# An encoder block on one core: x loaded over two queues, transposed blocks paired differently in PSUM, four gate sigmoids and one weight cut moved

## The chip, the cores and the metric

The kernel runs on one core of a Trainium2 chip. The metric is device microseconds of one execution, taken as the median of several runs. A separate profiled execution gives the trace from which all durations below come. Engine names: PE is TensorE's matmul side and PEld its weight load, DVE is VectorE, ACT is ScalarE, POOL is GpSimd and SP is SyncE, which only issues transfers here.

## The reference

One layer with sequence length 256 and model width 1024, all in float32:

```python
h = rmsnorm(x, norm_gain)
a_in, a_gate, q, k, v, b_gp, g_logits = split(h @ w_in)          # 1024 -> 8192 columns
y_a = (multiscale_pool(a_in, w_pool, pool_scale) * silu(a_gate)) @ w_proj_a
y_b = (dilated_attention(q, k, v, rel_bias) * silu(b_gp)) @ w_proj_b
gates = sigmoid(g_logits + b_gate)                               # two gates of 1024 columns
merged = gates[0] * y_a + gates[1] * y_b
y = rmsnorm(x + merged @ w_out, final_gain)
```

`multiscale_pool` takes centred means over windows of 2, 4, 8 and 16 positions in four groups of 128 channels, subtracts the token and multiplies each group by its own 128 x 128 matrix. The attention has 24 heads of 64 in three groups with different dilation; the eight heads of a group are merged over the groups by their softmax denominators.

## The kernel before, in words

**Exact products from rounded halves.** PE multiplies in a rounded 32-bit type (fp32r). To keep float32 accuracy every operand is cut into a high part (a rounding copy, `whi` for weights, `hh` for activations) and a low part (the rest, `wlo`, `hl`), and every product is three matmuls: high by high, low by high and high by low (`mm3`, lines 246 to 249). The high part of a weight tile is written by ACT (line 128), its low part by DVE (line 133); both are done in `cut_half`, half a tile at a time, two tiles ahead of the matmuls that use it. Weights come from DRAM in 41 tiles of `order` (lines 82 to 90), mostly 1 MB, through four raw buffers (`wraw`) on SP's queue; there are three buffers of `whi` and `wlo`, so the ACT copy of tile n waits until PE has finished tile n-3. The tile of kind `pool` holds the four 128 x 128 matrices; its halves have 2 x 128 columns each, and line 130 cuts its low part into four pieces of 128 x 128.

**The head (lines 68 to 243).** Its instructions on ACT, DVE, PE and POOL run in the order in which they are written. X, 256 rows by 1024, is loaded as two row blocks of 128 rows (512 KB each), both from SP's queue and ahead of the weights; the parameters `prm` come on ACT's queue. For each row block b, ACT and DVE each sum the squares of one half (lines 185, 187), DVE adds the sums (line 190), POOL takes the power -1/2 (line 191), and DVE and ACT scale one half of the row block each into `XN` (lines 194, 195). DVE then makes the high part of weight tile 0 in two halves (line 197), and POOL its low part in two pieces (lines 199, 200). `turn(kc, b)` transposes channel block kc (128 of the 1024 channels) of row block b on PE. The results go to four PSUM tiles `tps[0]` to `tps[3]`, one bank each, and every bank holds two channel blocks: kc and kc + 4 (line 204). For each kc, ACT reads the block from PSUM and writes its high part `hh` (line 223), and DVE reads the same block and `hh` and writes the low part `hl` (line 224). Between these, PE runs the first projection (`part0`, 16 matmuls for each of the three products): the product with `hl[kc]` two steps behind that with `hh[kc]`; then, when all of `hl` is used, the product with `wlo` with three small bias matmuls in between (line 237). PE's first matmul after the head is that of line 247.

**The long middle.** `heads` projects k, q and v, `project_t` gives one accumulator per 128 output channels from three PSUM banks (`mmb`, tag "mm"), and `step` (line 353) advances the attention: a scores stage `stage_s` (ends with an Exp on ACT, line 304), a transposing stage `stage_t` and an output stage `stage_o`. The latter ends with an ACT copy (line 344) and two DVE additions (lines 345, 346) that empty a single PSUM bank `op`. Outside the head the order on each engine is laid down when the program is built: an instruction that comes earlier in the text goes first if the builder's own model takes it to be ready; dependencies can be added by hand. `behind` adds such a dependency: a Sigmoid never goes ahead of the latest `stage_o` copy traced before it, because Exp and Sigmoid lie in different tables of ACT.

**The end of the middle.** Eight gate tiles (`gate_tile`, line 565) give the gate logits: tiles 0 to 3 fill `GA`, branch A's gate, tiles 4 to 7 branch B's. Each tile has two accumulators, each copied out by ACT (line 572), a `cut_half` and a `step`. After gate tile 6 come four pooling products (`mx`, line 595) and their scaling on DVE (line 597), the split of their result (lines 600, 601), a cut of the next weight tile and gate tile 7. Then the remaining attention steps run, and `squash` (line 604) applies Sigmoid in place to the two halves of `GA`, line 606. Branch A (`branch`, line 613) forms eight accumulators `y`; DVE multiplies each by its block of `GA` (`done_a`, line 629), which frees the PSUM bank that the third next accumulator needs. Branch B, the output product, the residual and the final norm follow.

Of the kernel before, what the change touches and what calls it, by code (L numbers as in the profile page):

```python
# [11 lines left out]
F32 = mybir.dt.float32  # L12
F32R = mybir.dt.float32r
AF = mybir.ActivationFunctionType
ALU = mybir.AluOpType
PSUM = bass.MemoryType.PSUM

P = 128
# [24 lines left out]
def encoder_block(ctx: ExitStack, tc: tile.TileContext, x, w_in, lines, w_pool, w_proj_a, w_proj_b,  # L43
                  w_out, final_gain, params, out):
    nc = tc.nc
    x2 = x[0]
# [6 lines left out]
    def slot(shape, dt, tag, name, bufs=1):  # L53
        return sb.tile(shape, dt, tag=tag, name=name, bufs=bufs)
# [6 lines left out]
    def bank(shape, tag, name, bufs):  # L61
        return ps.tile(shape, F32, tag=tag, name=name, bufs=bufs)
# [4 lines left out]

    X = slot([P, 2, D], F32, "v", "X", 2)
    for b in range(2):
        nc.sync.dma_start(X[:, b, :], x2[b * P:(b + 1) * P, :])  # L70
    ident = sb.tile([P, P], F32, name="ident")
    make_identity(nc, ident)
    mhalf = sb.tile([P, 1], F32, name="mhalf")
# [8 lines left out]
    order = []  # L82
# [12 lines left out]
    def load_next():  # L95
        n = state["load"]
        if n >= len(order):
            return
        kind, c = order[n]
        if kind == "in":  # L100
            src, shp = w_in[c // 256], [8, 256]
        elif kind == "pool":
            src, shp = w_pool, [4, 128]
        else:
            src, shp = {"pa": w_proj_a, "pb": w_proj_b, "out": w_out}[kind][c], [4, 512]
        t = slot([P] + shp, F32, "wraw", f"wraw{n}", NRAW)
        if n == 0:
            for h in range(2):
                k = shp[0] // 2
                nc.sync.dma_start(t[:, h * k:(h + 1) * k, :], src[:, h * k:(h + 1) * k, :])  # L110
        else:
            nc.sync.dma_start(t, src)
        raws[n] = (t, shp)
        state["load"] = n + 1

    def cut_half():
        n, h = divmod(state["cut"], 2)
        if n >= len(order):
            return
        t, shp = raws[n]  # L120
        if h == 0:
            parts[n] = (slot([P] + shp, F32R, "whi", f"whi{n}", 3), slot([P] + shp, F32R, "wlo", f"wlo{n}", 3))
            if n:
                load_next()
        hi, lo = parts[n]
        k = shp[0] // 2
        s = slice(h * k, (h + 1) * k)
        nc.scalar.activation(hi[:, s, :], t[:, s, :], AF.Copy)  # L128

        m = (k + 1) // 2 if 9 <= n <= 18 or n >= 24 else k  # L130
        for q in range(h * k, (h + 1) * k, m):
            s = slice(q, q + m)
            nc.vector.tensor_tensor(lo[:, s, :], t[:, s, :], hi[:, s, :].bitcast(F32), op=ALU.subtract)  # L133
        state["cut"] += 1

    def cut_next():
        cut_half()
        cut_half()

    def weights(n):  # L140
        return parts.pop(n)
# [13 lines left out]
    XN = slot([P, 2, D], F32, "v", "XN", 2)  # L155
# [5 lines left out]
    def cut_lo(n, k0, k1, eng):  # L161
        t, (hi, lo) = raws[n][0], parts[n]
        return eng.tensor_tensor(lo[:, k0:k1, :], t[:, k0:k1, :], hi[:, k0:k1, :].bitcast(F32), op=ALU.subtract)

    def open_parts(n):
        shp = raws[n][1]
        parts[n] = (slot([P] + shp, F32R, "whi", f"whi{n}", 3), slot([P] + shp, F32R, "wlo", f"wlo{n}", 3))
        state["cut"] = 2 * n + 2

    with tc.manual_schedule(engines={mybir.EngineType.Activation, mybir.EngineType.DVE, mybir.EngineType.PE,  # L170
                                    mybir.EngineType.Pool}):
        tiny = sb.tile([P, 1], F32, name="tiny")
        warm = sb.tile([P, P], F32, name="warm")
        nc.vector.memset(warm, 0.0)
        nc.scalar.activation(tiny, warm[:, 0:1], AF.Square)

        def keep_warm(times):
            for _ in range(times):
                nc.tensor.matmul(misc[:, P:2 * P], warm, warm, start=True, stop=True)

        keep_warm(WARM)
        halves = [slice(h * 512, (h + 1) * 512) for h in range(2)]
        for b in range(2):
            sq = [slot([P, 512], F32, "st", f"sq{b}{h}", 3) for h in range(2)]
            nc.scalar.activation(sq[0], X[:, b, halves[0]], AF.Square, scale=1.0 / 32.0, accum_out=ss[:, b, 0:1])
            xb = X[:, b, halves[1]]
            nc.vector.tensor_tensor_reduce(sq[1], xb, xb, scale=1.0 / D, scalar=EPS, op0=ALU.mult, op1=ALU.add,
                                           accum_out=ss[:, b, 1:2])
            t = slot([P, 1], F32, "rt", f"rt{b}", 2)
            nc.vector.tensor_tensor(t, ss[:, b, 0:1], ss[:, b, 1:2], op=ALU.add)  # L190
            nc.gpsimd.tensor_tensor(rs[:, b:b + 1], t, mhalf, op=ALU.pow)
        open_parts(0)
        for b in range(2):
            nc.vector.tensor_scalar(XN[:, b, halves[0]], X[:, b, halves[0]], rs[:, b:b + 1], None, op0=ALU.mult)
            nc.scalar.activation(XN[:, b, halves[1]], X[:, b, halves[1]], AF.Copy, scale=rs[:, b:b + 1])
        for k in (0, 4):
            nc.vector.tensor_copy(parts[0][0][:, k:k + 4, :], raws[0][0][:, k:k + 4, :])

        cut_lo(0, 0, 5, nc.gpsimd)
        first_lo = cut_lo(0, 5, 8, nc.gpsimd)  # L200
        tps = [bank([P, 2, S], "mm" if i < 3 else "T", f"tp{i}", 3 if i < 3 else 2) for i in range(4)]

        def turn(kc, b):
            nc.tensor.transpose(tps[kc % 4][:, kc // 4, b * P:(b + 1) * P], XN[:, b, kc * P:(kc + 1) * P], ident)

        acc = bank([P, 2, 512], "S", "k00", 1)
        acc0 = [acc[:, u, 0:S] for u in range(2)]

        def part0(kc, x):
            hi_, lo_ = parts[0]  # L210
            for u in range(2):
                c = slice(u * P, (u + 1) * P)
                nc.tensor.matmul(acc0[u], (lo_ if x == 2 else hi_)[:, kc, c], (hl if x == 1 else hh)[:, kc, :],
                                 start=x == 0 and kc == 0, stop=x == 2 and kc == KC - 1)

        for kc in range(KC):
            turn(kc, 0)
        for kc in range(KC):
            turn(kc // 2 + kc % 2 * 4, 1)
        for kc in range(KC):  # L220
            v = tps[kc % 4][:, kc // 4]
            gcol = prm[:, kc:kc + 1]
            nc.scalar.activation(hh[:, kc, :], v, AF.Copy, scale=gcol)
            nc.vector.scalar_tensor_tensor(hl[:, kc, :], v, gcol, hh[:, kc, :].bitcast(F32), op0=ALU.mult,
                                           op1=ALU.subtract)
            part0(kc, 0)
            if kc >= 2:
                part0(kc - 2, 1)
        for kc in (6, 7):
            part0(kc, 1)  # L230
        for kc in range(KC):
            if kc == 5:

                for t in range(3):
                    w = 3 * NH
                    o = 3 * P + t // 2 * w
                    nc.tensor.matmul(misc[:, t * w:(t + 1) * w], oh[:, t * P:(t + 1) * P], oh[:, o:o + w],
                                     start=True, stop=True)
            part0(kc, 2)
        cut_next()  # L240
        nc.vector.tensor_copy(line.rearrange("p i r h -> p r i h"),
                              misc[:, 0:LROW * NH].rearrange("p (r i h) -> p r i h", i=2, h=4))
        cut_next()
# [14 lines left out]
    def project_t(hi, lo, cb, name):  # L258
        acc = mmb(name)
        c = slice(cb * P, (cb + 1) * P)  # L260
        for kc in range(KC):
            mm3(acc, hi[:, kc, c], lo[:, kc, c], hh[:, kc, :], hl[:, kc, :], kc == 0, kc == KC - 1)
        return acc
# [111 lines left out]
    n = 0  # L375

    def heads(I, parts_):
        nonlocal n
        for part in parts_:
            for g in range(NG):  # L380
                hi, lo = weights(n) if n else (None, None)
                for u in range(2):
# [46 lines left out]
                    if n:  # L429
                        cut_half()  # L430
# [67 lines left out]
    for dst in ("u", "a", "b"):  # L498
        for t in range(2):
            hi, lo = weights(n)  # L500
# [61 lines left out]
    GA = GG[:, 0:8]  # L562
    GB = [GG[:, 8 + i] for i in range(4)]

    def gate_tile(t):
        nonlocal n
        hi, lo = weights(n)
        for u in range(2):
            cb = (2 * t + u) % 8
            acc = project_t(hi, lo, u, f"g{t}{u}")  # L570
            i = 8 + 2 * t + u
            nc.scalar.activation(GA[:, cb] if t < 4 else GB[cb], acc, AF.Identity, bias=prm[:, i:i + 1])
            cut_half()
            step()
        n += 1
# [28 lines left out]
    def squash(G):  # L604
        for g in G:
            behind(nc.scalar.activation(g, g, AF.Sigmoid), last_exp[0])

    gate_tile(7)
    while live:
        step()  # L610
    squash((GA[:, 0:4], GA[:, 4:8]))

    def branch(src_h, src_l, done):
        nonlocal n
# [208 lines left out]
```

## Time and profile before

| | |
|---|---|
| median of 3 runs | 260.43 us (260.27 to 260.70) |
| the profiled execution's own time | 260.82 us |
| its span | 259.0 us |
| PE busy | 250.4 us in 2160 matmuls |
| DVE busy | 210.2 us |
| ACT busy | 164.4 us |
| POOL busy | 74.5 us |
| memory read and written | 47.42 MB and 1.09 MB |
| granted PE clock | 0.995 of full speed over the span |

How to read it: the span goes from the first to the last instruction of the profiled execution, and 1.82 us of its own time lie outside. A row of the timeline gives the start in us, the duration in us, engine, line, operation, output<-inputs, shape and the count of merged instructions; in square brackets stands how long the engine had been idle before it and what ended that. Durations of neighbours on one engine overlap: the copy of line 223 lasts 0.47 us, but the next one begins 0.36 to 0.39 us after it. A row of the waits names who waited for whom, then the total, the times and the longest in us.

### The profile page before, as it was taken

How to read it: one execution, taken by the hardware profiler on the slowest of the kernel's cores; microseconds unless marked ns; L12 is line 12 of the kernel's file. 1: busy time of each engine (PE TensorE's matmuls, PEld its weight loads, DVE VectorE, ACT ScalarE, POOL GpSimd, SP SyncE). 2: the span in 40 equal slices, each digit the busy share in tenths (PEclk: the TensorE clock that was granted, in tenths of full speed). 3: DMA queues.
4: the chain of work that ended last, by engine and by line, in shares of the span. 5: the costliest groups of instructions: out<-in, count | busy, mean ns of one | idle time of the engine just before them, and what ended most of it. 6: DMA issues, size and time to landing. Idle time of an engine off the chain costs nothing.

```text
span 259.0 us, 5482 instructions
## 1 busy us (share of the span) xinstructions
PE 250.4 (97%) x2160; PEld 248.8 (96%) x2160; DVE 210.2 (81%) x412; ACT 164.4 (63%) x285; POOL 74.5 (29%) x101
## 2 busy tenths in 40 slices
PE   7899999999999999999999999999999999999990
PEld 7899999999999999999999999999999999999990
DVE  2899988778888787889697997967859988899383
ACT  4878577565666565658967777765457797446141
POOL 1563386002798000010763910000010020442011
PEclk9999999999999999999999999999999999999998
DMA  6999999984445553444989867144440696300022
GB/s 231 393 412 363 239 323 329 313 306 162 166 162 172 235 172 156 162 164 162 284 254 257 278 216 273 47 164 162 164 162 6 209 383 233 148 4 0 0 84 81
DMA packets 9992, 52.01 MB, mean 201 GB/s; under 512 B 1147, under 2 KB 2142, under 8 KB 4718
## 3 DMA queue, kind: packets, MB, share of 16 engines
q1 hardware_dynamic: 7022, 44.08, 48.4%
q0 software_dynamic: 2512, 7.12, 11.1%
q10 hardware_dynamic: 432, 0.46, 0.5%
q8 instruction: 17, 0.28, 0.4%
q14 instruction: 9, 0.07, 0.1%
HBM read 47.42 MB, written 1.09 MB: 187 GB/s over the span
## 4 chain that ended last, share of the span: by engine, by line
PE 84%; DVE 6%; issue 3%; ACT 2%; DMA 2%; POOLq 0%; POOL 0%; SPq 0%; DVEq 0%; ACTq 0%
PE v L249 4%; PE v L248 4%; PE q L249 4%; PE q L248 4%; PE v L247 4%; PE q L247 4%; PE g L247 4%; PE g L248 4%; PE g L249 4%; PE k L247 4%; PE k L249 4%; PE k L248 4%; PE y L247 2%; PE y L248 2%; PE y L249 2%
## 5 line engine op out<-in xcount | busy, mean ns | idle before, releaser
L133 DVE TENSOR_TENSOR wlo<-wraw,whi 128x512 fp32r<-128x512 f32 (+2 forms) x134 | 108.5, 849 | 8.3 <-ACT whi L128 7.3
L128 ACT ACTIVATE whi<-wraw 128x1024 fp32r<-128x1024 f32 (+1 forms) x80 | 81.0, 1038 | 23.2 <-PE q L248 10.1
L247 PE MATMUL g<-hh,whi 128*128 128x256 f32 x128 | 35.8, 280 | 0.0
L249 PE MATMUL g<-hh,wlo 128*128 128x256 f32 x128 | 35.4, 277 | 0.0
L248 PE MATMUL g<-hl,whi 128*128 128x256 f32 x128 | 35.4, 276 | 0.0
L304 ACT ACTIVATE st<-st,nm 128x512 f32<-128x512 f32 x16 | 11.6, 722 | 29.6 <-DVE nm L301 29.6
L247 PE MATMUL v<-whi,hh 128*128 128x256 f32 x96 | 26.6, 277 | 0.0
L249 PE MATMUL v<-whi,hl 128*128 128x256 f32 x96 | 26.5, 276 | 0.0
L248 PE MATMUL v<-wlo,hh 128*128 128x256 f32 x96 | 26.5, 276 | 0.0
L249 PE MATMUL q<-hh,wlo 128*128 128x256 f32 x96 | 26.5, 276 | 0.0
L247 PE MATMUL q<-hh,whi 128*128 128x256 f32 x96 | 26.5, 276 | 0.0
L248 PE MATMUL q<-hl,whi 128*128 128x256 f32 x96 | 26.5, 276 | 0.0
L247 PEld LDWEIGHTS g<-hh,whi 128*128 128x128 f32 x128 | 24.0, 188 | 0.1
L248 PEld LDWEIGHTS g<-hl,whi 128*128 128x128 f32 x128 | 24.1, 188 | 0.0
L249 PEld LDWEIGHTS g<-hh,wlo 128*128 128x128 f32 x128 | 24.0, 188 | 0.0
L247 PE MATMUL k<-hh,whi 128*128 128x256 f32 x80 | 22.2, 277 | 0.0
L249 PE MATMUL k<-hh,wlo 128*128 128x256 f32 x80 | 22.1, 277 | 0.0
L248 PE MATMUL k<-hl,whi 128*128 128x256 f32 x80 | 22.1, 277 | 0.0
L248 PEld LDWEIGHTS v<-wlo,hh 128*128 128x128 f32 x96 | 18.0, 188 | 0.0
L249 PEld LDWEIGHTS q<-hh,wlo 128*128 128x128 f32 x96 | 18.0, 188 | 0.0
L248 PEld LDWEIGHTS q<-hl,whi 128*128 128x128 f32 x96 | 18.0, 188 | 0.0
L247 PEld LDWEIGHTS q<-hh,whi 128*128 128x128 f32 x96 | 18.0, 188 | 0.0
(177 smaller groups left out, 760.2 us busy)
## 6 DMA issues: line engine op xcount, KB each, us to landing
wraw<-in_w_in_dram SPq DMA_DIRECT2D x31, 1024.0 KB, 6.4
wraw<-in_w_out_dram SPq DMA_DIRECT2D x4, 1024.0 KB, 4.9
T<-line_d POOLq DMA_DIRECT2D x4, 576.0 KB, 6.8
KX<-KX POOLq DMA_DIRECT2D x8, 256.0 KB, 14.5
wraw<-in_w_proj_a_dram SPq DMA_DIRECT2D x2, 1024.0 KB, 4.7
wraw<-in_w_proj_b_dram SPq DMA_DIRECT2D x2, 1024.0 KB, 4.9
X<-in_x_dram SPq DMA_DIRECT2D x2, 512.0 KB, 4.2
wraw<-in_w_in_dram SPq DMA_DIRECT2D x2, 512.0 KB, 6.6
```

Source lines behind the costliest of these rows:

```text
L128: nc.scalar.activation(hi[:, s, :], t[:, s, :], AF.Copy)
L133: nc.vector.tensor_tensor(lo[:, s, :], t[:, s, :], hi[:, s, :].bitcast(F32), op=ALU.subtract)
L247: nc.tensor.matmul(acc, ah, bh, start=first, stop=False)
L248: nc.tensor.matmul(acc, ah, bl, start=False, stop=False)
L249: nc.tensor.matmul(acc, al, bh, start=False, stop=last)
L304: e = nc.scalar.activation(st, st, AF.Exp, bias=nm, scale=-1.0, accum_out=l)
```

## The change

Five places change.

1. Row block 1 of X is issued by ACT, row block 0 by SP as before. ACT issues it ahead of `prm`.
2. The transposes of channel blocks 2j and 2j + 1 go to the same PSUM tile `tps[j]`; before, kc and kc + 4 shared one.
3. The transposes of row block 1 are issued in the order 0 to 7; before, in the order 0, 4, 1, 5, 2, 6, 3, 7, in which banks are finished one by one.
4. The low part of the tile of kind `pool` is written by POOL, all others by DVE as before.
5. `squash` of branch A's gate stands ahead of gate tile 7 and the last attention steps, not behind them.

```diff
     for b in range(2):
-        nc.sync.dma_start(X[:, b, :], x2[b * P:(b + 1) * P, :])
+        (nc.sync, nc.scalar)[b].dma_start(X[:, b, :], x2[b * P:(b + 1) * P, :])
...
         t, shp = raws[n]
+        kind = order[n][0]
...
-            nc.vector.tensor_tensor(lo[:, s, :], t[:, s, :], hi[:, s, :].bitcast(F32), op=ALU.subtract)
+            (nc.gpsimd if kind == "pool" else nc.vector).tensor_tensor(lo[:, s, :], t[:, s, :],
+                                                                       hi[:, s, :].bitcast(F32), op=ALU.subtract)
...
-            nc.tensor.transpose(tps[kc % 4][:, kc // 4, b * P:(b + 1) * P], XN[:, b, kc * P:(kc + 1) * P], ident)
+            nc.tensor.transpose(tps[kc // 2][:, kc % 2, b * P:(b + 1) * P], XN[:, b, kc * P:(kc + 1) * P], ident)
...
         for kc in range(KC):
-            turn(kc // 2 + kc % 2 * 4, 1)
+            turn(kc, 1)
         for kc in range(KC):
-            v = tps[kc % 4][:, kc // 4]
+            v = tps[kc // 2][:, kc % 2]
...
+    squash((GA[:, 0:4], GA[:, 4:8]))
     gate_tile(7)
     while live:
         step()
-    squash((GA[:, 0:4], GA[:, 4:8]))
```

## The prediction

> **What bounds the kernel now.** I read the page's busy shares and the chain that ended last, then PE's waits, then the timeline of the head and of the end of the middle.
>
> ```profile
> PE 250.4 (97%) x2160; PEld 248.8 (96%) x2160; DVE 210.2 (81%) x412; ACT 164.4 (63%) x285; POOL 74.5 (29%) x101
> PE 84%; DVE 6%; issue 3%; ACT 2%; DMA 2%; POOLq 0%; POOL 0%; SPq 0%; DVEq 0%; ACTq 0%
> PE tp L204 <- DVE XN L194: 1.2, 1, 1.2
> PE op L330 <- DVE ATT L346: 0.2, 1, 0.2
> ```
>
> PE works nearly all the time and makes most of the chain. From its first matmul behind the head (line 247) it runs on with three short holes, priced below. So whatever delays that matmul delays the end by as much, unless a later hole takes it up, and these holes hang on PE's own earlier results and move with it. The change has two places: the head, whose length counts one for one, and the holes around gate tile 7.
>
> **The head: how its end is made.**
>
> ```profile
> 9.10 0.69 DVE L197 CAST whi<-wraw 128x1024 fp32r<-128x1024 f32 x1 [0.41 <-DMA wraw<-in_w_in_dram]
> 8.74 3.13 ACT L223 ACTIVATE hh<-tp,prm 128x256 fp32r<-128x256 f32 x8 [0.42 <-PE tp L204]
> 9.71 3.22 DVE L224 SCALAR_TENSOR_TENSOR hl<-tp,prm,hh 128x256 fp32r<-128x256 f32 x8
> 9.71 0.48 DVE L224 SCALAR_TENSOR_TENSOR hl<-tp,prm,hh 128x256 fp32r<-128x256 f32 x1
> 10.22 0.87 ACT L223 ACTIVATE hh<-tp,prm 128x256 fp32r<-128x256 f32 x2
> 11.39 0.48 ACT L223 ACTIVATE hh<-tp,prm 128x256 fp32r<-128x256 f32 x1
> 9.87 4.79 POOL L163 TENSOR_TENSOR wlo<-wraw,whi 128x1280 fp32r<-128x1280 f32 x2 [2.30 <-DVE whi L197]
> 12.62 0.86 PE L213 MATMUL k<-hl,whi 128*128 128x256 f32 x6
> 13.32 1.32 PE L213 MATMUL k<-hh,wlo 128*128 128x256 f32 x10
> 15.07 0.93 PE L213 MATMUL k<-hh,wlo 128*128 128x256 f32 x6
> 15.83 0.28 PE L247 MATMUL k<-hh,whi 128*128 128x256 f32 x1
> ```
>
> DVE's eight `hl` start at 9.71, when its second cast is done, which had waited for the load of weight tile 0. They follow each other every 0.39 us ((3.22 - 0.48) / 7) and end at 12.93. PE's last six products with `hl` start at 12.62, one per 0.117 us, the last two (for block 7) at 13.09; then come the low weight products, and line 247 at 15.83. POOL's low part ends at 14.66, before PE needs its second piece at 15.07: not the bound. The end of `hl` is.
>
> **Neighbouring blocks in a bank.** In these rows `hh` of block 4 starts at 10.22, just behind `hl` of block 0 (9.71 + 0.48 = 10.19), and the last `hh` at 11.39 stands equally behind `hl` of block 3 (9.71 + 3 x 0.39 + 0.48 = 11.36). Blocks 0 and 4 share a PSUM bank, 3 and 7 too. The first projection tile shows the same with nothing else in common:
>
> ```profile
> 19.20 0.85 DVE L428 TENSOR_TENSOR K<-k,K 64x256 fp32r<-64x256 f32 x2
> 20.08 0.77 ACT L426 ACTIVATE K<-k 64x256 fp32r<-64x256 f32 x2 [0.95 <-DVE K L428]
> ```
>
> ACT's read of the second half of accumulator `k00` waits until DVE has read the first half, 0.03 us after its end. I conclude that reads of one PSUM tile by ACT and DVE are kept in the order of the text. The old layout lets this cost nothing: `hh` of block kc + 4 is behind `hl` of block kc, four steps earlier. In the new one `hh` of block 1 is behind `hl` of block 0, and `hl` of block 1 is behind that `hh`. Worked out from a first `hl` at H: it ends at H + 0.48; `hh` 1 runs from H + 0.51 to H + 0.98; `hl` 1 starts at H + 1.01; `hh` 2, in the next bank, follows `hh` 1 by 0.38 ((3.13 - 0.48) / 7) and ends at H + 1.37; `hl` 2 starts at H + 1.40. A pair takes 1.40 us instead of 0.78. The last `hl` starts at H + 3 x 1.40 + 1.01 = H + 5.21 and ends at H + 5.69 instead of H + 3.22. With H as before that is 15.40; PE's last two products start at 15.43 instead of 13.09: 2.34 us later, and nothing between there and line 247 gets shorter. Behind the waiting `hh` on ACT stand the copies of weight tile 1 (line 128), behind the `hl` on DVE that tile's low part; both slip by some 2 us, but PE wants them from line 247 on, which slips as far. [...] The new order of the transposes spares `hh` 0 the ACT half of `XN`, but `hl` 0 waits for the cast, so this is worth nothing.
>
> **X over two queues.**
>
> ```profile
> 0.74 0.85 SPq L70 DMA_DIRECT2D X<-in_x_dram  x2
> prm<-in_params_dram ACTq DMA_DIRECT2D x1, 64.0 KB, 3.9
> 3.00:4.00 1.00, 1.00 (x7) 1.00 (x7) 0.00 (x0) 0.00 (x0) 0.00 (x0) 1.00 1.03 395
> 6.00:7.00 1.00, 0.03 (x1) 0.00 (x0) 0.90 (x4) 1.00 (x3) 0.33 (x2) 1.00 0.73 221
> 4.50 0.69 DVE L187 CUSTOM_DVE_ANT_0 sq<-X 128x512 f32<-128x512 f32 x1 [3.50 <-DMA X<-in_x_dram]
> 5.31 0.16 DVE L190 TENSOR_TENSOR rt<-ss 128x1 f32<-128x1 f32 x1
> 5.80 0.69 DVE L187 CUSTOM_DVE_ANT_0 sq<-X 128x512 f32<-128x512 f32 x1 [0.33 <-DMA X<-in_x_dram]
> 7.60 0.49 DVE L194 TENSOR_SCALAR XN<-X,rs 128x512 f32<-128x512 f32 x1 [0.45 <-POOL rs L191]
> 8.01 0.69 DVE L197 CAST whi<-wraw 128x1024 fp32r<-128x1024 f32 x1
> ```
>
> (The two window rows end in the share of the 16 DMA engines and GB/s.) While X comes in, the DMA engines are full (1.03, 395 GB/s), so a second queue brings no bytes. Row block 0 landed by 4.50, row block 1 by 5.80. The 64 KB of `prm`, issued at 0.74 on ACT's queue, needed until 4.64, as long as the 512 KB beside it: I take it that the queues take turns row by row. Then both row blocks land at about 5.6 to 5.8, the first 1.1 us later than now. The work on them then bunches: DVE's second sum starts 0.9 us behind the first (4.50 to 5.31 and the 0.16 behind it, less overlap), at 6.5 instead of 5.8, and everything down to `XN` of row block 1 is 0.7 later: 8.3 instead of 7.60. The casts follow at 8.71 and 9.32 (by 0.41 and 0.61, as now); the second no longer waits for its load (9.10). H is 9.93 instead of 9.71: 0.2 us lost. The bounds: a gain of 0.4, all of the second cast's wait, if tile 0, now issued 0.43 us sooner, fills the slack at 6 to 7 us (221 GB/s); a loss of 0.4, if row block 1, with `prm` behind it, lands 0.2 later still. I take 0.2 lost. [...]
>
> ACT's issue of X takes 0.4 us ahead of `prm` and its table load, which must only be over by 4.5. In all the head grows by 2.34 + 0.2 = 2.5 us (1.9 to 2.8).
>
> **Pool low parts on POOL.**
>
> ```profile
> 186.14 0.89 DVE L133 TENSOR_TENSOR wlo<-wraw,whi 128x128 fp32r<-128x128 f32 x4
> 187.97 0.42 DVE L346 TENSOR_TENSOR ATT<-ATT,op 64x256 f32<-64x256 f32 x1
> 188.10 0.28 PE L249 MATMUL g<-hh,wlo 128*128 128x256 f32 x1
> 188.54 0.47 PE L330 MATMUL op<-pp,VS 128*128 128x256 f32 x2 [0.16 <-DVE ATT L346]
> 188.47 0.73 POOL L634 TENSOR_TENSOR ATT<-ATT,SB 128x256 f32<-128x256 f32 x1 [38.26 <-DVE ATT L346]
> ```
>
> PE's output stage waits for line 346, which empties its bank; it starts at 188.54, where 0.11 behind the matmul at 188.10 was due: 0.33 lost. Four low parts, 0.89 us, stand ahead of that on DVE. Without them the hole closes. POOL, idle for 38 us there, needs 0.4 to 0.7 us a piece (half of or all of its 0.73), under 3 us, and the `mx` products want them 13 us later. Should POOL slow DVE beside it, the gain shrinks to 0. Gain 0.33 (0 to 0.33).
>
> **Sigmoids ahead of gate tile 7.**
>
> ```profile
> 196.85 0.37 ACT L344 ACTIVATE ATT<-op 64x256 f32<-64x256 f32 x1
> 199.02 1.06 ACT L128 ACTIVATE whi<-wraw 128x1024 fp32r<-128x1024 f32 x1 [1.80 <-PE g L248]
> 199.98 0.46 ACT L572 ACTIVATE G<-g,prm 128x256 f32<-128x256 f32 x1
> 200.49 0.38 PE L247 MATMUL mx<-PHL,whi 128*128 128x256 f32 x1
> 208.92 1.28 ACT L606 ACT_TABLE_LOAD   x1
> 210.21 2.01 ACT L606 ACTIVATE GG<-GG 128x1024 f32<-128x1024 f32 x2
> 211.37 0.28 PE L249 MATMUL y<-AMH,wlo 128*128 128x256 f32 x1
> 211.79 0.39 PE L247 MATMUL y<-AMH,whi 128*128 128x256 f32 x1
> ```
>
> Now the table load and the sigmoids come behind the last attention copy and make PE wait for a bank of `y`: 211.79 where 211.48 was due, 0.31 lost. Moved, they hang on the copy at 196.85, and ACT is idle from 197.22 to 199.02. I expect the table load and the first sigmoid there (1.28 + 1.04, to 199.5) and the second behind the next copies; the copy of gate tile 6 (now 199.98), for whose bank the third `mx` product waits, then comes no later than now. Gain 0.31. What it costs if the cover is gone is the first rival. No later work on ACT needs the Exp table. Both middle edits: 0.64 gained.
>
> **The sum.** 2.54 - 0.64 = 1.9 us longer. The profiled execution took 260.82 us, its span and 1.82 outside it; it would become 262.7. It stands 0.39 above the median of 260.43, so the median becomes 262.3.
>
> **The rivals.** (1) Both sigmoids go into ACT's gap ahead of the copy of gate tile 6: ACT is then busy to 197.22 + 1.28 + 2.01 = 200.5, the weight copy and that copy end 1.5 us later than now, and PE stands still as long before the third `mx` product. Their pull forward by program order speaks for it, the 1.80 us gap, too short for both, against. 262.3 + 1.5 = 263.8; it decides from the moment that the builder's model sees 2 us of idle ACT or more. (2) Turns at the DMA engines do not harm: X lands as now, and tile 0 sooner; H is 0.4 earlier than now, the head grows by 1.9 only: 261.7. The slack at 6 to 7 us speaks for it, `prm`'s landing against. (3) The other side: ACT and DVE are not ordered on a bank where both only read. The place is lines 223 and 224, the price 2.34 us, and it decides from the second block on: without this wait the head loses 0.2 and the middle gains 0.64, 260.0, no different from now, or 259.4 with case 2. The rows at 10.22, 11.39 and 20.08 speak against.
>
> **How the numbers follow.** Forecast 0.65, rival 1 0.17, rival 2 0.11, rival 3 0.07. Forecast: 262.3, by the bounds 261.7 (head 1.9, middle 0.64) to 263.2 (head 2.8, middle nothing). The range of 261.5 to 263.8 takes in rival 2, with a further 0.1 to 0.2 should the small hole at the third `mx` product close too, and rival 1 up to its price. What a measurement here can tell from no change is 0.2%, 0.5 us. Only rival 3 is not slower by that: 0.03 faster, 0.04 same, 0.93 slower.
>
> **What would show it.** `hl` at uneven steps (about 1.0 and 0.4 us in turn) with ACT waiting on DVE at line 223 four times; line 247 starting 2 to 3 us later; the first sum of squares after 5.4; no wait at line 330 for line 346; the table load near 197 plus the head's delay, and no hole in `y`. Evenly spaced `hl` every 0.39 us would make the prediction wrong, as would a hole over 1 us at `mx`.

## The result, and the profile after

The changed kernel takes 263.77 us (median of 4 runs, 263.60 to 263.95); before, on the same chip, takes 260.56 us (4 runs, 260.27 to 260.74). The ratio is 1.0122, 95% interval 1.0108 to 1.0135: 2.8 to 3.5 us slower, where 1.9 was forecast. The profiled execution took 263.63 us with a span of 261.8. The line numbers of the changed kernel are one or two higher: 223 is 225, 224 is 226, 247 is 249, 330 is 332, 346 is 348, 572 is 574, 606 is 608, 629 is 631.

PE's waits, in the columns of the first view shown above:

```profile
PE k L215 <- ACT hh L225: 1.3, 4, 0.5
PE mx L249 <- ACT G L574: 0.5, 1, 0.5
PE op L332 <- DVE ATT L348: 0.2, 1, 0.2
```

Two rows are new: the first projection waits four times for `hh`, and a pooling product waits for the copy of a gate tile. The wait at the output stage, which was to go, is still there. The timeline of the head after:

```profile
5.63 0.69 DVE L189 CUSTOM_DVE_ANT_0 sq<-X 128x512 f32<-128x512 f32 x1 [4.63 <-DMA X<-in_x_dram]
8.61 1.35 DVE L199 CAST whi<-wraw 128x1024 fp32r<-128x1024 f32 x2
9.54 0.47 ACT L225 ACTIVATE hh<-tp,prm 128x256 fp32r<-128x256 f32 x1 [0.55 <-PE tp L206]
10.05 0.48 DVE L226 SCALAR_TENSOR_TENSOR hl<-tp,prm,hh 128x256 fp32r<-128x256 f32 x1
10.57 0.84 ACT L225 ACTIVATE hh<-tp,prm 128x256 fp32r<-128x256 f32 x2 [0.55 <-DVE hl L226]
11.08 0.87 DVE L226 SCALAR_TENSOR_TENSOR hl<-tp,prm,hh 128x256 fp32r<-128x256 f32 x2 [0.54 <-ACT hh L225]
...
12.49 0.87 DVE L226 SCALAR_TENSOR_TENSOR hl<-tp,prm,hh 128x256 fp32r<-128x256 f32 x2 [0.54 <-ACT hh L225]
...
15.33 0.48 DVE L226 SCALAR_TENSOR_TENSOR hl<-tp,prm,hh 128x256 fp32r<-128x256 f32 x1 [0.54 <-ACT hh L225]
15.35 0.50 PE L215 MATMUL k<-hh,whi 128*128 128x256 f32 x2 [0.24 <-ACT hh L225]
15.69 0.86 PE L215 MATMUL k<-hl,whi 128*128 128x256 f32 x6
18.88 0.28 PE L249 MATMUL k<-hh,whi 128*128 128x256 f32 x1
```

ACT and DVE hand each bank to and fro: `hh` waits for `hl` and `hl` for `hh`, and a pair takes 1.41 us (11.08 to 12.49). Row block 0 lands at 5.63 instead of 4.50, the first `hl` starts at 10.05 instead of 9.71, and PE's first matmul behind the head at 18.88 instead of 15.83: 3.05 us, nearly all that the kernel lost. The end of the middle after, from the same view:

```profile
188.79 1.84 POOL L134 TENSOR_TENSOR wlo<-wraw,whi 128x128 fp32r<-128x128 f32 x4 [35.81 <-ACT whi L129]
191.01 0.42 DVE L348 TENSOR_TENSOR ATT<-ATT,op 64x256 f32<-64x256 f32 x1
191.59 0.47 PE L332 MATMUL op<-pp,VS 128*128 128x256 f32 x2 [0.17 <-DVE ATT L348]
199.90 0.37 ACT L346 ACTIVATE ATT<-op 64x256 f32<-64x256 f32 x1
200.28 1.28 ACT L608 ACT_TABLE_LOAD   x1
201.58 2.01 ACT L608 ACTIVATE GG<-GG 128x1024 f32<-128x1024 f32 x2
203.49 0.46 ACT L574 ACTIVATE G<-g,prm 128x256 f32<-128x256 f32 x1
204.00 0.39 PE L249 MATMUL mx<-PHL,whi 128*128 128x256 f32 x1 [0.52 <-ACT G L574]
217.35 0.41 DVE L631 TENSOR_TENSOR GG<-y,GG 128x256 f32<-128x256 f32 x1
217.40 0.28 PE L251 MATMUL y<-AMH,wlo 128*128 128x256 f32 x1
217.81 0.38 PE L249 MATMUL y<-AMH,whi 128*128 128x256 f32 x1
```

Both sigmoids stand ahead of the copy of gate tile 6 (203.49), and the third `mx` product waits for it. The first hole of `y` is gone, but a later `y` product starts 0.41 us behind its predecessor (217.40, 217.81), 0.30 more than the 0.11 between neighbours: it waits for the bank that DVE empties at 217.35 + 0.41.

### The profile page after: what moved, and what is told of

It reads as the page before. It is cut to its first block, busy times and chain, and to the rows that moved or that the text cites. A ratio compares the mean times of both kernels' runs of the same rounds, so it can differ in the third digit from the quotient of the medians.

```text
span 261.8 us, 5480 instructions
## 1 busy us (share of the span) xinstructions
PE 251.4 (96%) x2160; PEld 249.2 (95%) x2160; DVE 207.8 (79%) x408; ACT 164.9 (63%) x285; POOL 75.0 (29%) x105
## 5 line engine op out<-in xcount | busy, mean ns | idle before, releaser
L134 DVE TENSOR_TENSOR wlo<-wraw,whi 128x512 fp32r<-128x512 f32 (+1 forms) x130 | 105.1, 847 | 9.7 <-ACT whi L129 8.9
L251 PEld LDWEIGHTS v<-whi,hl 128*128 128x128 f32 x96 | 18.0, 188 | 0.0
```

The costliest lines, as they stand in the source:

```text
L134: (nc.gpsimd if kind == "pool" else nc.vector).tensor_tensor(lo[:, s, :], t[:, s, :], hi[:, s, :].bitcast(F32), op=ALU.subtract)
L251: nc.tensor.matmul(acc, al, bh, start=False, stop=last)
```

## The experiments

The theory after these traces (A): the text order of reads of one PSUM tile makes the pairing cost 2.6 to 2.8 us, X over two queues costs a few tenths, the moved sigmoids cost a few tenths at `mx`, and the low parts on POOL are worth nothing. Its rivals stand in the expectations. All times are medians in us beside the kernel before on the same chip; unless a diff says otherwise, a kernel is the one before with that edit.

| kernel | this | before | ratio, 95% interval |
|---|---|---|---|
| pairing alone | 263.14 | 260.61 | 1.0101, 1.0088 to 1.0114 |
| X over two queues alone | 261.46 | 260.61 | 1.0039, 1.0025 to 1.0054 |
| sigmoids alone | 260.95 | 260.61 | 1.0011, 1.0003 to 1.0020 |
| low parts on POOL alone | 260.56 | 260.61 | 0.9997, 0.9989 to 1.0006 |
| pairing, other text order | 260.65 | 260.45 | 1.0007, 0.9998 to 1.0016 |
| X in column halves | 261.32 | 260.45 | 1.0045, 1.0020 to 1.0071 |
| one sigmoid ahead, one behind | 260.78 | 260.45 | 1.0015, 1.0006 to 1.0024 |
| all but the pairing | 261.49 | 260.45 | 1.0046, 1.0029 to 1.0064 |
| sigmoid tied to gate tile 7 | 260.14 | 260.35 | 0.9986, 0.9977 to 0.9994 |
| `prm` ahead of row block 1 | 263.80 | 260.35 | 1.0113, 1.0096 to 1.0130 |
| `prm` late, X on one queue | 266.65 | 260.35 | 1.0227, 1.0202 to 1.0252 |
| the change mended | 260.17 | 260.35 | 0.9988, 0.9978 to 0.9998 |

### The pairing alone (edits 2 and 3)

```diff
-            nc.tensor.transpose(tps[kc % 4][:, kc // 4, b * P:(b + 1) * P], XN[:, b, kc * P:(kc + 1) * P], ident)
+            nc.tensor.transpose(tps[kc // 2][:, kc % 2, b * P:(b + 1) * P], XN[:, b, kc * P:(kc + 1) * P], ident)
...
-            turn(kc // 2 + kc % 2 * 4, 1)
+            turn(kc, 1)
...
-            v = tps[kc % 4][:, kc // 4]
+            v = tps[kc // 2][:, kc % 2]
```

> Only the pairing of the channel blocks and the order of the transposes are changed (edits 2 and 3). Theory A, ordered reads of one bank: the first low part hl starts at about 9.7 us as in the kernel before, the eight come in steps of about 1.0 and 0.4 us in turn, ACT waits for DVE four times at 0.55 us, and PE's first matmul behind the head starts 2.7 us later than in the kernel before (2.54 from the longer chain and 0.2 from PE's own products queued behind the last hh); the time grows by 2.6 to 2.8 us. Theory B, the pairing costs little and the loads of X are what lengthened the head: the time grows by less than 1 us.

Measured: 2.53 us slower by the medians. Its timeline:

```profile
10.68 0.87 DVE L224 SCALAR_TENSOR_TENSOR hl<-tp,prm,hh 128x256 fp32r<-128x256 f32 x2 [0.54 <-ACT hh L223]
12.09 0.88 DVE L224 SCALAR_TENSOR_TENSOR hl<-tp,prm,hh 128x256 fp32r<-128x256 f32 x2 [0.54 <-ACT hh L223]
...
18.54 0.28 PE L247 MATMUL k<-hh,whi 128*128 128x256 f32 x1
```

The first `hl` is as before (9.65), the pairs step by 1.41 us, line 247 starts 2.71 us later than before. So the pairing makes most of the loss by itself.

### The pairing with both copies ahead of both differences

Beside the edits 2 and 3:

```diff
-        for kc in range(KC):
-            v = tps[kc // 2][:, kc % 2]
-            gcol = prm[:, kc:kc + 1]
-            nc.scalar.activation(hh[:, kc, :], v, AF.Copy, scale=gcol)
-            nc.vector.scalar_tensor_tensor(hl[:, kc, :], v, gcol, hh[:, kc, :].bitcast(F32), op0=ALU.mult,
-                                           op1=ALU.subtract)
+        for kc in range(0, KC, 2):
+            two = [(k, tps[k // 2][:, k % 2], prm[:, k:k + 1]) for k in (kc, kc + 1)]
+            for k, v, gcol in two:
+                nc.scalar.activation(hh[:, k, :], v, AF.Copy, scale=gcol)
+            for k, v, gcol in two:
+                nc.vector.scalar_tensor_tensor(hl[:, k, :], v, gcol, hh[:, k, :].bitcast(F32), op0=ALU.mult,
+                                               op1=ALU.subtract)
```

> Neighbouring channel blocks in a bank as in the change (edits 2 and 3), but in the text both copies hh of a bank stand ahead of both differences hl. Theory A (the pairing costs its 2.5 us only because reads of one PSUM tile by ACT and DVE are kept in the order of the text, which in the change alternates hh, hl, hh, hl): now hl of a bank waits only for the second hh of that bank, one copy later (about 0.4), and hl then run at an even 0.39 to 0.45; the first hl at 9.7 to 10.1, the last ends 13.0 to 13.4, line 247 of PE starts 0 to 0.5 later than before, the time is before's 0 to +0.5. Rival B (two engines that read one bank hinder each other in the hardware, whatever the order): hl stay at pairs of 1.4 or single ones get longer than 0.48, line 247 is 2 to 3 later, +2 us or more.

Measured: 260.65 against 260.45, no difference that the interval can show (at most 0.4 us of the 2.5 are left). ACT's eight copies and DVE's eight differences run without a stop again:

```profile
8.63 3.02 ACT L223 ACTIVATE hh<-tp,prm 128x256 fp32r<-128x256 f32 x8 [0.30 <-PE tp L204]
9.76 3.22 DVE L225 SCALAR_TENSOR_TENSOR hl<-tp,prm,hh 128x256 fp32r<-128x256 f32 x8
```

The banks are shared as in the change; only the order in the text differs, and the loss is gone. ACT's second copy of the first bank ends at about 9.5, before DVE is there (9.76), so DVE does not wait for the grouping. The rival, that the hardware slows two readers of a bank, falls as an account of the loss: with the pairing alone a single `hl` lasts 0.48 and a single `hh` 0.47 as before, and the lost time is waits. What two reads of one bank at the same moment would cost no run here shows: the waits keep them apart.

### X over two queues alone (edit 1)

```diff
-        nc.sync.dma_start(X[:, b, :], x2[b * P:(b + 1) * P, :])
+        (nc.sync, nc.scalar)[b].dma_start(X[:, b, :], x2[b * P:(b + 1) * P, :])
```

> Only X goes over two queues (edit 1). Theory A, the queues take turns and row block 0 lands as late as row block 1: first sum of squares at 5.6 us instead of 4.5, first hl at 10.0 instead of 9.71, PE's first matmul behind the head 0.3 us later, the time 0.2 to 0.4 us longer. Rival: the chain of the old layout absorbs it, since PE's products with hl run behind DVE anyway: same time within 0.1 us.

Measured: 0.85 us slower by the medians, more than either expected, and over a wider spread (260.73 to 262.42). Of its trace, the issues (KB each, us from issue to landing) and the timeline:

```profile
X<-in_x_dram ACTq DMA_DIRECT2D x1, 512.0 KB, 4.8
prm<-in_params_dram ACTq DMA_DIRECT2D x1, 64.0 KB, 7.3
```

```profile
5.37 0.69 DVE L187 CUSTOM_DVE_ANT_0 sq<-X 128x512 f32<-128x512 f32 x1 [4.37 <-DMA X<-in_x_dram]
9.59 0.69 DVE L197 CAST whi<-wraw 128x1024 fp32r<-128x1024 f32 x1 [0.56 <-DMA wraw<-in_w_in_dram]
10.20 3.22 DVE L224 SCALAR_TENSOR_TENSOR hl<-tp,prm,hh 128x256 fp32r<-128x256 f32 x8
```

Both row blocks land together at 5.4, as the prediction had it. What it had not: weight tile 0 lands later too (the second cast waits to 9.59, before 9.10), although it was issued sooner. And `prm` now lands 7.3 us after its issue at 1.19.

Which of these cost the time is read from PE, at its first products with `hh`. With the edit, then in the kernel before:

```profile
9.81 1.23 PE L213 MATMUL k<-hh,whi 128*128 128x256 f32 x6
```

```profile
9.27 1.24 PE L213 MATMUL k<-hh,whi 128*128 128x256 f32 x6
```

From there to line 247 PE takes 6.66 us (to 16.47), before 6.56 (to 15.83), and the waits have none of PE for `hl` in either kernel. So in the old layout the end of the head hangs on the first `hh` (9.28, before 8.74). This waits for the transposes (first at 7.93, before 7.21), and they wait for row block 0, which lands 0.87 later (5.37 instead of 4.50): the bunching made 0.54 of the 0.64 that line 247 lost. The late tile 0 moved the first `hl`, but PE comes to it only at 10.88, 0.20 behind its end (10.20 + 0.48) and 1.07 behind PE's first product with `hh`, the same as before (10.34 less 9.27).

### X in column halves over both queues

```diff
-        nc.sync.dma_start(X[:, b, :], x2[b * P:(b + 1) * P, :])
+        for h, q in enumerate((nc.sync, nc.scalar)):
+            q.dma_start(X[:, b, h * 512:(h + 1) * 512], x2[b * P:(b + 1) * P, h * 512:(h + 1) * 512])
```

> Both queues carry X, but both take halves of the same row block (512 columns each), row block 0 first. Theory A (the queues take turns, and the harm of the change is that the two row blocks then land together): row block 0 lands as before, at about 4.5, row block 1 at 5.8, first sum of squares at 4.5 to 4.7, first hl at 9.7 to 9.9, the time is before's -0.2 to +0.3. Rival B (the second queue itself harms: its issue on ACT ahead of prm, or prm and weight tile 0 landing later): the first sum of squares is in time, but the second cast of line 197 waits for its load as with the change (load at 9.59 against 9.10), first hl at 10.1 or later, +0.4 or more.

Measured: 0.87 us slower by the medians.

```profile
4.25 0.69 DVE L188 CUSTOM_DVE_ANT_0 sq<-X 128x512 f32<-128x512 f32 x1 [3.26 <-DMA X<-in_x_dram]
9.77 0.69 DVE L198 CAST whi<-wraw 128x1024 fp32r<-128x1024 f32 x1 [0.55 <-DMA wraw<-in_w_in_dram]
10.91 0.50 PE L214 MATMUL k<-hl,whi 128*128 128x256 f32 x2 [0.40 <-DVE hl L225]
```

Theory A misses here, and rival B's signs come. Row block 0 lands early (4.25), nothing bunches, the first `hh` starts at 8.75 as before, and the time is lost all the same, by another way: weight tile 0's second cast comes 0.67 later than before, and now PE waits 0.40 for the first `hl`. So a late tile 0 can cost as much as the bunching. It does not clear the bunching in edit 1, where PE has no such wait: this kernel took one cost away and put another in its place.

### `prm` ahead of row block 1, and `prm` late with X on one queue

Two kernels ask whether the 64 KB of `prm`, pushed back beside tile 0, make tile 0 late. The first is edit 1 with `prm` issued first on ACT's queue:

```diff
+    prm = sb.tile([P, NPRM], F32, name="prm")
+    nc.scalar.dma_start(prm, params)
     X = slot([P, 2, D], F32, "v", "X", 2)
     for b in range(2):
-        nc.sync.dma_start(X[:, b, :], x2[b * P:(b + 1) * P, :])
+        (nc.sync, nc.scalar)[b].dma_start(X[:, b, :], x2[b * P:(b + 1) * P, :])
...
-    prm = sb.tile([P, NPRM], F32, name="prm")
-    nc.scalar.dma_start(prm, params)
```

The second keeps X on SP's queue and issues `prm` behind ACT's first square:

```diff
-    nc.scalar.dma_start(prm, params)
...
             nc.scalar.activation(sq[0], X[:, b, halves[0]], AF.Square, scale=1.0 / 32.0, accum_out=ss[:, b, 0:1])
+            if b == 0:
+                nc.scalar.dma_start(prm, params)
```

> Edit 1 alone, but with the issue of prm ahead of row block 1 on ACT's queue. Theory A (the later landing of weight tile 0 comes from the 64 KB of prm: behind row block 1 they take turns with tile 0 instead of with X): the second cast of line 197 starts at 9.1 to 9.3, first hl at 9.8 to 10.0, the time is before's +0.0 to +0.4. Rival B (the second queue as such delays what follows X on SP's queue): the second cast waits for its load to 9.5 or later, first hl at 10.1 to 10.3, +0.4 to +0.9.

> X on one queue as before; only prm is issued later, on ACT's queue behind the first square of line 185 (at about 5.1 instead of 0.74), so that its 64 KB come beside weight tile 0. Theory A (prm beside tile 0 delays tile 0's landing): the second cast of line 197 starts at 9.4 to 9.8 as with edit 1 alone, although X comes over one queue; first sum of squares at 4.3 to 4.5; +0.3 or more, and more still if prm lands after 8.7, when hh wants it. Rival B (it is the second queue of X): the second cast starts at 9.0 to 9.2; then a delay comes only from hh waiting for prm.

Measured: 3.45 and 6.30 us slower. With `prm` ahead, the timeline, then a window of 1 us (its last three columns are PE's granted clock, the share of the DMA engines and GB/s):

```profile
8.76 0.69 DVE L187 CUSTOM_DVE_ANT_0 sq<-X 128x512 f32<-128x512 f32 x1 [3.31 <-DMA X<-in_x_dram]
10.18 2.93 PE L204 MATMUL tp<-ident,XN 128*128 128x128 f32 x16 [4.04 <-DVE XN L194]
```

```profile
12.00:13.00 1.00, 1.00 (x7) 1.00 (x6) 0.88 (x3) 1.00 (x3) 0.66 (x1) 0.50 0.95 385
```

With `prm` late, the timeline and the issues:

```profile
9.48 0.69 DVE L198 CAST whi<-wraw 128x1024 fp32r<-128x1024 f32 x1 [0.59 <-DMA wraw<-in_w_in_dram]
12.85 3.02 ACT L224 ACTIVATE hh<-tp,prm 128x256 fp32r<-128x256 f32 x8 [4.86 <-DMA prm<-in_params_dram]
```

```profile
prm<-in_params_dram ACTq DMA_DIRECT2D x1, 64.0 KB, 8.6
```

The first fits neither theory: row block 1, issued at 1.18 but behind `prm`, landed at 8.76, 7.6 us after its issue, and tile 0's casts behind it could no longer show anything. The second answers: X on one queue, and tile 0's second cast at 9.48, where the eight traces with X on one queue and `prm` ahead, the kernel before among them, have 9.03 to 9.20. So issuing `prm` late is enough to delay tile 0 by 0.3 to 0.4 in this one execution, without a second queue for X, as theory A had it. Most of the 6.30 is `hh`'s wait for `prm`: `hh` starts at 12.85 instead of 8.74, 4.11 later, and PE's first matmul behind the head 6.20 later (22.03). The rest goes with PE's granted clock, 0.50 in the window from 12 to 13 us, and with products that up to 18.2 us came at 0.43 us for two (14.82 to 15.25) instead of 0.22 (10.59 to 10.81; last section).

How the two queues share the engines is read from the DMA packets, counted over all 16 engines (q1 is SP's queue and q10 is ACT's; each row gives packets, MB and share of the engines). With edit 1 alone, from 5.5 to 6.5 us, SP's queue moves rows of 4 KB and ACT's the rows of 512 B of `prm`:

```profile
q1 hardware_dynamic: 50, 0.20, 77.0%
q10 hardware_dynamic: 52, 0.03, 9.0%
```

With `prm` late, from 4.2 to 8.5 us, this is all that moved:

```profile
q1 hardware_dynamic: 352, 1.33, 92.5%
```

While both have work, the packets come about one for one (50 and 52 in the first two rows). But `prm`, issued at 4.13 (ACT waited for it from 7.99 to 12.85), moved no packet from 4.2 to 8.5 us. So half of its 8.6 us is a wait for the first packet. What holds that back stays open, and so does how a load that moves only from 8.5 on delays a tile that is cast at 9.48. Counts over 16 engines cannot tell turns by single rows from turns by several rows, so no run here shows the size of a turn.

### The low parts on POOL alone (edit 4)

```diff
-            nc.vector.tensor_tensor(lo[:, s, :], t[:, s, :], hi[:, s, :].bitcast(F32), op=ALU.subtract)
+            (nc.gpsimd if kind == "pool" else nc.vector).tensor_tensor(lo[:, s, :], t[:, s, :],
+                                                                       hi[:, s, :].bitcast(F32), op=ALU.subtract)
```

> Only the low parts of the pool weights go to POOL (edit 4). Theory A, the 0.89 us that DVE saves goes to other DVE work that the build then puts ahead of the addition PE waits for: the hole of 0.33 us at the output stage stays, the time is the same within 0.15 us. Rival: on its own, without the other edits, the hole closes: 0.3 us shorter.

Measured: 260.56 against 260.61, the same. Its timeline:

```profile
185.77 1.84 POOL L134 TENSOR_TENSOR wlo<-wraw,whi 128x128 fp32r<-128x128 f32 x4 [34.30 <-ACT whi L129]
185.81 0.63 DVE L312 TENSOR_SCALAR st<-st,rl 128x384 f32<-128x384 f32 x1
187.26 0.69 DVE L303 CUSTOM_DVE_ANT_1 st<-sp,BT 128x512 f32<-128x512 f32 x1
187.99 0.43 DVE L348 TENSOR_TENSOR ATT<-ATT,op 64x256 f32<-64x256 f32 x1
```

DVE has lost 0.89 us of work ahead of line 348 (before: 346, at 187.97), and this still starts at 187.99; PE's wait behind it is 0.17, as before. The time went to two things: the reduction of line 303 (before: 301, 0.69 us), which used to stand behind and now stands ahead, and line 312 (before: 310), which takes 0.63 instead of 0.42 beside POOL's work. The first is the larger part.

### The sigmoids: alone, split, and tied to gate tile 7

All of edit 5 alone:

```diff
+    squash((GA[:, 0:4], GA[:, 4:8]))
     gate_tile(7)
...
-    squash((GA[:, 0:4], GA[:, 4:8]))
```

The first half ahead of gate tile 7, the second behind it:

```diff
+    squash((GA[:, 0:4],))
     gate_tile(7)
...
-    squash((GA[:, 0:4], GA[:, 4:8]))
+    squash((GA[:, 4:8],))
```

The first half between the two copies of gate tile 7, with a dependency on the first of them (`squash` is moved up and takes what to stay behind):

```diff
-            nc.scalar.activation(GA[:, cb] if t < 4 else GB[cb], acc, AF.Identity, bias=prm[:, i:i + 1])
+            copy = nc.scalar.activation(GA[:, cb] if t < 4 else GB[cb], acc, AF.Identity, bias=prm[:, i:i + 1])
+            if t == 7 and u == 0:
+                squash((GA[:, 0:4],), copy)
...
-    squash((GA[:, 0:4], GA[:, 4:8]))
+    squash((GA[:, 4:8],))
```

> Only the sigmoids of branch A's gate stand ahead of gate tile 7 (edit 5). Theory A, both sigmoids fill ACT's gap: a hole of about 0.7 us at the third pooling product instead of 0.12, the hole of 0.31 at the fourth product y goes, another opens at a later y where DVE is late; together 0.1 to 0.4 us longer. Rival: the sigmoids are worth their 0.31 us and the hole at the pooling product came from the late head: 0.2 to 0.4 us shorter.

> The sigmoids are halved: the first half (gates 0 to 3) ahead of gate tile 7, the second half behind it. Theory A (a sigmoid costs when it stands ahead of the copy of gate tile 6 or behind the last gate tile; table load and one sigmoid, 1.28 + 1.0, fit beside PE's work between): the hole of 0.31 at y is gone or under 0.1, the hole at the third mx product is no more than 0.2 larger than before; the time is before's -0.4 to -0.1. Rival B (table load and one sigmoid already stand ahead of the copy, 2.3 us of work on ACT in a gap of 1.8): the mx hole is 0.5 or more and the time is before's +0.1 to +0.5, as with both sigmoids moved.

> The old layout and queues; the first half of the sigmoids is tied behind the first copy of gate tile 7 on ACT (so neither it nor the table load can go ahead of the copies of gate tile 6), the second half stays behind gate tile 7. Theory A (only the place of table load and sigmoids against gate tile 6's copy made the loss of 0.3; two sigmoids behind gate tile 7 made the hole of 0.31 at y): no wait over 0.2 at mx, table load at about 205, no hole at y; the time is before's -0.4 to -0.1. Rival B (the hole at y is a backlog of ACT and DVE that any place of the sigmoids leaves, since ACT's 3.3 us must be done in any case): a hole of 0.3 or more at some y product stays, the time is before's -0.1 to +0.3.

Measured: 0.34 slower, 0.33 slower, 0.21 faster. Alone, the third `mx` product waits as in the changed kernel. Split, one sigmoid goes into the gap and the weight copy, which edit 5 had pushed behind the gate copy, stands ahead of it again:

```profile
198.75 1.06 ACT L606 ACTIVATE GG<-GG 128x1024 f32<-128x1024 f32 x1
199.71 1.04 ACT L128 ACTIVATE whi<-wraw 128x1024 fp32r<-128x1024 f32 x1
200.66 0.45 ACT L572 ACTIVATE G<-g,prm 128x256 f32<-128x256 f32 x1
201.17 0.39 PE L247 MATMUL mx<-PHL,whi 128*128 128x256 f32 x1 [0.52 <-ACT G L572]
```

So my theory of the split fell, to its rival: about 1 us of work more or less in the gap gives the same wait, since the builder fills the place. Tied, the copy of gate tile 6 is in time, and the table load goes where ACT has room:

```profile
199.93 0.45 ACT L576 ACTIVATE G<-g,prm 128x256 f32<-128x256 f32 x1
204.93 1.28 ACT L567 ACT_TABLE_LOAD   x1
```

Behind the head the only wait of PE that is left is the one at the output stage, and no `y` product starts more than 0.23 behind its predecessor. The hole of 0.31 that the prediction wanted to close is closed, by a place that the change does not use. This version beats both kernels, by 0.14% (interval 0.06 to 0.23%) over the kernel before.

### All but the pairing, and the change mended

The first is the changed kernel with the old layout of the banks. The second has the pairing with the other text order, the low parts on POOL and the tied sigmoid, with X on one queue; its edits stand above.

> All of the change but the pairing (edits 1, 4 and 5). Theory A (the parts add up, since they lie in different stages): X over two queues +0.85 (+0.5 by its trace), sigmoids +0.35, low parts 0: +0.8 to +1.2 us over before; the changed kernel is then 2.0 to 2.4 longer than this. Rival B (the pairing covers part of the delay of X, since DVE's casts and the wait for a bank share the time): this is +0.5 or less and the pairing's share in the change is over 2.6.

> The change with what theory A says makes its losses taken out: pairs of neighbouring blocks with both hh ahead of both hl in the text, low parts of the pooling tile on POOL, the first half of the sigmoids tied behind the first copy of gate tile 7, X on one queue. Theory A: pairs +0.1, low parts 0, sigmoids -0.3: before's -0.4 to +0.1. Rival B (the hole at y is not closed by another place): 0 to +0.4.

Measured: 1.04 slower and 0.18 faster. By the ratios the pairing adds 0.0076 to the rest (1.0122 less 1.0046), 2.0 us; alone it costs 0.0101, 2.6 us. With intervals of 0.0013 to 0.0018 on either side of each ratio the runs cannot tell these two apart: the parts add up as far as they show. In the traces line 249 starts at 16.27 without the pairing and at 18.88 with it. The 16.27 is 0.44 later than in the kernel before; the first `hh` is 0.48 later (9.22), the first `hl` only 0.19 (9.90), so here too the old layout goes by `hh`. The mended change is no faster than the tied sigmoid alone: of the five edits only the aim of the fifth was worth anything.

## Why the prediction was right and where it was not

**The range held in part by luck.** The forecast was 1.9 us more and the measurement is 3.2, and 263.77 lies just under the upper end of 263.8. That end stood for rival 1's hole of 1.5 us with the head as forecast. The time came there by other sums: a head 0.5 longer than forecast, and a middle that lost 0.6 where 0.64 was to be gained.

**The head's mechanism was right for the pairing.** Reads of one PSUM tile are kept in text order; the steps of `hl`, the four waits of ACT and the pair of 1.40 us (measured 1.41) came as worked out. The reordered text settles it: same banks, and at most 0.4 us by its interval. Rival 3, that there is no such order, is out.

**For the old head it was not.** "The end of `hl` is" the bound, said the prediction. But in its own rows the last `hl` ends at 12.93 and PE comes to its products at 13.09, and PE has no wait between its first product with `hh` (9.27) and line 247 (15.83). The old head hangs on the first `hh`. The pairing pushes `hl` far behind that, so its price does not suffer; the price of X does.

**The pairing's price, 2.34, was mis-sized: 2.7.** The failed step is "PE's last two products start at 15.43". I let them follow the last `hl`. But PE takes the products in the order of the text, and the last two `hh` products stand ahead: they wait for the last `hh`, start 0.02 behind the last `hl` (15.35 and 15.33 after), and then six `hl` products, not two, are still to do (15.69, x6). The last two start at 15.69 + 4 x 0.114 = 16.15; by my formula, with the first `hl` at H = 10.05, they were due at H + 5.72 = 15.77. The 0.38 between is the missing price.

**X, 0.2 lost, was mis-sized.** In the changed kernel the casts came nearly as worked out (8.61, forecast 8.71) and did not wait for the load. But the first `hl` stands 0.04 behind the end of the first `hh` (9.54 + 0.47), which waits for the transposes: I had taken the cast for the last in line, and it was `hh`. That makes 0.34. Alone the edit cost more, 0.65 to 1.4 us by its interval, and there the failed step is again "The end of `hl` is": with the old layout the loss is that of the first `hh`, 0.54, and not that of the first `hl`. Line 247 came 0.64 later. The step "the second no longer waits for its load" failed too: tile 0 was to land in time, and its second cast waited to 9.59 (9.29 in the kernel with all but the pairing). PE did not wait for that with edit 1; in the column halves it did. Both row blocks landing together was right. Of the 0.85 the trace shows 0.64. Rival 2, harmless turns and 0.4 gained, is out.

**The low parts, -0.33, were worth 0.** The bound was given ("should POOL slow DVE beside it, the gain shrinks to 0"), but the larger part of the cause was another: the slower line 312 took 0.21, and taking work away let the builder put the reduction ahead of line 346 (0.69). I had named what would go and not asked what would come forward in its place.

**The sigmoids, -0.31, cost 0.3.** The failed step is "the second behind the next copies". Both went ahead of the copy of gate tile 6, as in rival 1. Its condition was wrong, as the gap was 1.80 us and it took 3.3 us of work; so was its price of 1.5: the copy came 0.46 later against the attention copy (203.49 less 199.90, before 199.98 less 196.85), because the builder put the weight copy of 0.95 behind it. The hole grew from 0.12 to 0.69. The gain at `y` was taken back at once by DVE, whose multiplication at 217.35 stands behind other work. In the kernel with all but the pairing this second hole does not occur, so it hangs on the order that the builder finds.

**The sum.** Head 3.05 instead of 2.54, middle about +0.6 by its holes instead of -0.64: 3.6 by these sums, 2.8 to 3.5 by the clock. Part of the difference is in the profiled executions: the 22.9 us from the first `y` to the first product of `both` before were 22.4 in the kernel with the reordered pairs, which has the same middle and the same hole. A stretch that long differs by 0.5 us from one execution to another, so single profiles could not settle any of the three small edits; the repeated runs did.

## What to carry to other kernels

Where two engines read one accumulator tile, look for the order in which the text lists their reads: alternating readers within one tile make a ping-pong (1.41 us a pair here, 2.53 us in all), and grouping each engine's reads cures it without touching the layout (0.20 us left by the medians, no difference by the interval). When work leaves an engine or a gap opens in a builder's order, ask what the builder will move into it; a dependency on the right neighbour places a long instruction better than its place in the text. Before you price a load that lands later, look where the busiest engine comes to its data: the old head hung on the first `hh`, and a later `hl` cost nothing until PE had to wait for it (0.49 us later and no wait with edit 1, a wait of 0.40 in the column halves). Count a small load on a second queue as part of the large loads' schedule: ahead of row block 1 the 64 KB landed 3.9 us after their issue, behind it 7.3, at 8.5 us, when both row blocks had been there since 5.4.

## What was not expected of the hardware

64 KB on ACT's queue took 3.9 us from issue to landing when issued together with X, 7.3 behind 512 KB on its own queue, and 8.6 when issued at 4.13, with nothing ahead of it on its own queue and weight tiles on SP's; 512 KB behind it took 7.6.

PE's granted clock was 0.50 in the window from 12 to 13 us with `prm` ahead, after PE had been idle for 4.04 us, and the first products took longer, six with `hh` 1.63 us instead of 1.24: part of what these two kernels lost. With `prm` late PE was idle for 4.35 us (to 13.37) and the clock was 0.50 in the same window; PE took 8.66 us from its first product with `hh` to the end of the head (13.37 to 22.03) where the kernel before takes 6.56. In the changed kernel PE idles for 1.2 us ahead of the transposes and the clock stays at 1.00. How long PE has to be idle for this, these three idle times do not show.

DVE's line 312 took 0.63 instead of 0.42 us while POOL subtracted; the next two DVE instructions, which read PSUM, kept their 0.41 and 0.42. DVE lost 0.21 us there, where one of POOL's four pieces lasts 0.46 (1.84 / 4); why, no run here shows.
